# Two early output stores in a tuned cumsum-difference matmul: issued ahead of the next transposes instead of last

## The chip, the cores and the metric

The kernel runs on one core of a Trainium2 chip. The metric is the device time of one execution in microseconds (us), lower is better. The kernel before takes 1458.15 us, the median of three runs that lie between 1458.01 and 1458.67 us.

## The reference, cut to what matters

```python
cs = np.cumsum(x, axis=1)                       # x: 8 x 2048 x 2048, float32
diff = cs - np.concatenate([zeros, cs[:, :-1, :]], axis=1)
return np.matmul(diff, w).astype(np.float32)    # w: 2048 x 2048, float32
```

The difference of a running sum is the input again, so the kernel computes x times w: 16384 rows of x, each 2048 long, times one 2048 x 2048 matrix.

## The kernel before, in words

**Tiling.** A row tile is 128 rows of x (x2, lines 112 and 487). There are 128 of them. The output row of a tile has four column blocks of 512; the left half of w has blocks 0 and 1, the right half blocks 2 and 3.

**First part.** Row tiles 0 to 3 are multiplied plainly, in bf16, while w arrives. `fetch` (L258) loads a stripe of w, `cast` (L266) narrows it, `plain` (L303) multiplies. The left half of the four tiles is finished first: `plain_out(0, r)` copies seven results out of PSUM (tile 3 gives one block there, the other comes from `left_over`). The first two, of tile 0, lie in the buffer F. The other five lie in the five `results` buffers o0 to o4: o0 and o1 are tile 1, o2 and o3 tile 2, o4 tile 3. All seven are noted in the list `done`, to be stored later by `put` (L313). Then the right half of w comes in, and its eight results are noted in a second list `done`; the five left-half stores that wait meanwhile are called `stored`.

**Second part.** From row tile 4 on the kernel works on groups of four tiles with sums and products of half and quarter blocks in fp16, so that fewer matmuls are needed. A tile takes these steps: two loads into F (`load`, L112; tile 5 alone comes by one DMA into the space of xP, L487), a sum of absolute values on ScalarE (`weigh`, L124), two tiny VectorE steps (`scale_of`, L141 and L143), narrowing to fp16 on ScalarE (`narrow`, L163), and two DMA transposes (`turn`, L176). Results leave by `keep` (ScalarE, L630) and `add` (VectorE, L633), and by `put` (L644).

**The first group of the second part** is `group_plain`, on tiles 4, 5, 6 and 7, called g, g + 1, h and h + 1 there. TensorE does, each as 16 matmuls of line 603: A11g x B11, A12g x B21, A11h x B11, A12h x B21, then S1g x T1, S2g x T2, S4g x B22, S3g x T3, then the same for h, beginning with S2h x T2. S1g is the sum of the two transposed halves of tile 5; it is made by VectorE (`total`, L593) and written to the tile S1, S2g from S1g and tile 4. S1h and S2h are the same for tiles 7 and 6. T1, T2 and T3 are differences of pieces of w (L505 and L585).

**Memory.** Everything in the block `with ExitStack() as head` gives its space back at the end of the first part. In the order of allocation these are the seven ring buffers of 2 KB per partition, the five results buffers o0 to o4 of 2 KB, and xP. Then the second part allocates in the same space seven buffers c0 to c6 of 2 KB, S1 of 4 KB and `inner` of 20 KB. S1 so lies where o0 and o1 lay, and `inner` where o2 to o4 and most of xP lay. Whoever writes S1 first must wait until the stores that read o0 and o1 have landed.

**The order of the work.** Every DMA of the kernel is issued by SyncE (SP), whose instructions run in the order of the program. The order is written out by hand: `after(engine, ...)` keeps each engine's instructions in the order of the calls. SP's DMAs use eight completion semaphores in turn, so a DMA waits, besides its data, until the DMA eight issues before it has landed. Around the change SP's order is: the last five stripes of w, two loads of tile 6, two stores from F, two transposes of tile 4 (L176), the load of tile 5 (L487), two right-half stores whose buffers are needed soon, two transposes of tile 6, two loads of tile 7, two transposes of tile 5, six right-half stores, the five left-half stores o0 to o4, the store of `left_over`, two loads of tile 8, two stores of tile 4's result, two transposes of tile 7.

Of the kernel before, what the change touches and what calls it, by code (L numbers as in the profile page):

```python
# [10 lines left out]
def kernel(  # L11
# [96 lines left out]
    def load(t, i):  # L108
        if t < END:
            after(  # L110
                "sp",
                lambda: nc.sync.dma_start(  # L112
                    where[t][i], x2[ds(t * P, P), ds(i * NH, NH)]
                ),
            )
# [69 lines left out]
    with ExitStack() as head:  # L185
# [126 lines left out]
        def put(c, rows, columns, queue=nc.gpsimd):  # L312
            return queue.dma_start(out2[rows, columns], c)  # L313
# [45 lines left out]
        done = []  # L359
# [76 lines left out]
            bring(ko)  # L436
        load(PLAIN + 2, 0)
        load(PLAIN + 2, 1)
        for c, rows, columns in done[:2]:
            put(c, rows, columns, nc.sync)  # L440
        stored = done[2:]
        done = []
        greatest_of_w(1)
        scale_of_w(1)
# [857 lines left out]
```

## Time and profile before

| what | value |
|---|---|
| median of three runs | 1458.15 us |
| the profiled execution, its own time | 1456.43 us |
| its span in the trace | 1454.4 us |
| mean granted TensorE clock | 0.998 |
| TensorE matmul busy | 1441.0 us |
| VectorE busy | 1318.1 us |
| ScalarE busy | 972.1 us |
| share of the 16 DMA engines of the one DMA queue that SP feeds | 86.0% |
| stores from the buffers o | 5, of 256 KB each, median 4.4 us from issue to landing |

The profile shows one execution of the program. PE is TensorE (PEld its weight loads), DVE VectorE, ACT ScalarE, POOL GpSimd, SP SyncE; SPq is the sequencer of SP, which issues the DMAs. A row of the timeline has the start in us from the start of the span, the duration, the engine, the line of the kernel, the operation, the tile written and the tile read, and how many instructions were merged; in brackets stands how long the engine was idle before and what ended that. A tile is named without its number: `o` stands for any of o0 to o4, `x` for any transposed half tile, `S` for S1. The chain of waits follows the work back from the last instruction to what released each step.

### The profile page before, as it was taken

How to read it: one execution, taken by the hardware profiler on the slowest of the kernel's cores; microseconds unless marked ns; L12 is line 12 of the kernel's file. 1: busy time of each engine (PE TensorE's matmuls, PEld its weight loads, DVE VectorE, ACT ScalarE, POOL GpSimd, SP SyncE). 2: the span in 40 equal slices, each digit the busy share in tenths (PEclk: the TensorE clock that was granted, in tenths of full speed). 3: DMA queues.
4: the chain of work that ended last, by engine and by line, in shares of the span. 5: the costliest groups of instructions: out<-in, count | busy, mean ns of one | idle time of the engine just before them, and what ended most of it. 6: DMA issues, size and time to landing. Idle time of an engine off the chain costs nothing.

```text
span 1454.4 us, 20187 instructions
## 1 busy us (share of the span) xinstructions
PE 1441.0 (99%) x6692; PEld 652.2 (45%) x6692; DVE 1318.1 (91%) x2309; ACT 972.1 (67%) x1473; POOL 42.9 (3%) x130
## 2 busy tenths in 40 slices
PE   8989999999999999999999999999999999999998
PEld 4434444444444444444444444444444444444443
DVE  5888899999999999999999999999999999999998
ACT  6967566676666666667666667766666766666662
POOL 0011000000000000000000000000000000000000
PEclk9999999999999999999999999999999999999999
DMA  9999788998888998878998888988878988889973
GB/s 364 345 253 291 200 214 238 249 247 234 234 232 241 246 253 230 237 236 232 260 242 231 219 242 239 261 234 243 227 232 244 250 238 235 229 241 247 254 201 124
DMA packets 378199, 351.58 MB, mean 242 GB/s; under 512 B 274800, under 2 KB 274800, under 8 KB 377968
## 3 DMA queue, kind: packets, MB, share of 16 engines
q1 hardware_dynamic: 378096, 350.31, 86.0%
q8 instruction: 52, 0.85, 0.2%
q14 instruction: 51, 0.42, 0.1%
HBM read 150.99 MB, written 134.22 MB: 196 GB/s over the span
## 4 chain that ended last, share of the span: by engine, by line
PE 93%; DMA 2%; DVE 2%; issue 1%; ACT 1%; SPq 0%; DVEq 0%; POOL 0%; ACTq 0%
PE b L622 61%; PE b L603 32%; DMA W<-in_w_dram 2%; ACT waste L272 1%; DVE c L633 1%; DVE W L341 0%; DMA out_dram<-o 0%; DVE W L505 0%; SPq L224 0%; ACT o L331 0%; DVE wb L333 0%; DVE x L333 0%; DVE W L585 0%; ACT F L163 0%; SPq L313 0%
## 5 line engine op out<-in xcount | busy, mean ns | idle before, releaser
L633 DVE SCALAR_TENSOR_TENSOR c<-b,of,c 128x512 f32<-128x512 f32 x790 | 573.6, 746 | 73.5 <-PE b L622 63.6
L603 PE MATMUL b<-W,x 128*128 128x512 f16 x2144 | 506.6, 379 | 0.0
L630 ACT ACTIVATE c<-b,of 128x512 f32<-128x512 f32 x492 | 313.2, 680 | 228.4 <-PE b L622 117.2
L622 PE MATMUL b<-W,x 128*128 128x512 f16 x1904 | 455.1, 379 | 0.0
L163 ACT ACTIVATE F<-F,of 128x1024 f16<-128x1024 f32 x246 | 282.3, 1148 | 178.6 <-DVE of L143 176.4
L622 PEld LDWEIGHTS <-x 128*128 128x128 f16 x2500 | 244.6, 98 | 295.9 <-issue 1.9
L603 PEld LDWEIGHTS <-x 128*128 128x128 f16 x2144 | 209.8, 98 | 253.0
L124 ACT ACTIVATE waste<-F 128x1024 uint8<-128x1024 f32 x246 | 259.2, 1054 | 4.8 <-DMA F<-in_x_dram 2.7
L622 PEld LDWEIGHTS <-inner 128*128 128x128 f16 x1644 | 160.9, 98 | 194.0
L622 PE MATMUL b<-W,inner 128*128 128x512 f16 x940 | 241.2, 379 | 0.0
L593 DVE TENSOR_TENSOR x<-x,x 128x1024 f16<-128x1024 f16 (+1 forms) x390 | 227.2, 583 | 3.2
L622 PE MATMUL b<-flow,x 128*128 128x512 f16 x588 | 150.9, 379 | 0.0
L622 PE MATMUL b<-inner 128*128 128x512 f16 x472 | 121.1, 379 | 0.0
L946 DVE TENSOR_TENSOR flow<-W 128x2048 f16<-128x2048 f16 x88 | 107.0, 1216 | 0.0
L1039 DVE TENSOR_TENSOR b<-b,c 128x512 f32<-128x512 f32 x116 | 80.4, 694 | 13.4 <-PE b L622 13.4
L149 POOL TENSOR_SCALAR of<-uw,of 128x2 f32<-128x2 f32 x124 | 41.7, 350 | 1307.1 <-DVE of L141 734.7
L946 DVE TENSOR_TENSOR flow<-W,inner 128x2048 f16<-128x2048 f16 x58 | 70.8, 1220 | 0.0
L1032 ACT COPY c<-b 128x512 f32<-128x512 f32 x58 | 33.4, 577 | 51.6 <-PE b L622 49.7
L303 PE MATMUL b<-wb,xP 128*128 128x512 bf16 x240 | 54.0, 379 | 2.0 <-DVE wb L266 1.3
L1032 ACT COPY b<-b 128x512 f32<-128x512 f32 x87 | 51.2, 589 | 0.0
L593 DVE TENSOR_TENSOR inner<-x 128x512 f16<-128x512 f16 x117 | 49.3, 421 | 2.0
L593 DVE TENSOR_TENSOR inner<-x,inner 128x512 f16<-128x512 f16 x117 | 49.2, 421 | 2.0
(66 smaller groups left out, 518.7 us busy)
## 6 DMA issues: line engine op xcount, KB each, us to landing
F<-in_x_dram SPq DMA_DIRECT2D x246, 512.0 KB, 5.2
out_dram<-c SPq DMA_DIRECT2D x492, 256.0 KB, 3.0
W<-in_w_dram SPq DMA_DIRECT2D x32, 512.0 KB, 8.8
W<-in_x_dram SPq DMA_DIRECT2D x16, 256.0 KB, 7.8
x<-F SPq DMA_TRANSPOSE x246, 3.3
out_dram<-wb SPq DMA_DIRECT2D x5, 256.0 KB, 3.5
out_dram<-o SPq DMA_DIRECT2D x5, 256.0 KB, 4.4
xP<-in_x_dram SPq DMA_DIRECT2D x1, 1024.0 KB, 4.8
```

What stands on the lines that cost most here:

```text
L124: lambda: nc.scalar.activation(waste, where[t][i], ABS, scale=1.0 / ROW, accum_out=sums_of[t][:, i : i + 1],),
L149: after("pool", lambda: nc.gpsimd.tensor_scalar(u, uw, m, None, MUL))
L163: lambda: nc.scalar.activation(narrowed(t)[:, ds(i * NH, NH)], where[t][i], COPY, scale=s),
L303: lambda: nc.tensor.matmul(ps[r][n], xP[:, r, ko, :], wb[h, ko][:, ds(n * NB, NB)], start=(ko == 0), stop=(ko == KO - 1),),
L593: after("dve", lambda: nc.vector.tensor_tensor(dst.all, p.all, q.all, op))
L603: said = nc.tensor.matmul(to[n], a[k], b[k][:, n, :], start=(first and k == 0), stop=(k == KH - 1), skip_group_check=True,)
L622: said = nc.tensor.matmul(to, a[k], b[k], start=(first and k == 0), stop=(k == 3), skip_group_check=True)
L630: after("act", lambda: nc.scalar.activation(c, p, COPY, scale=u))
L633: after("dve", lambda: nc.vector.scalar_tensor_tensor(c, p, u, c, MUL, ADD))
L946: after("dve", lambda: nc.vector.tensor_tensor(in_twos(flow), x, y, op))
L1032: after("act", lambda: nc.scalar.copy(c, p))
L1039: after("dve", lambda: nc.vector.tensor_tensor(t, p, s, ADD))
```

## The change

Of the seven left-half results, the kernel before stores two right after the loads of tile 6 and the five others at the end of the first part. The kernel after stores four there and three at the end. The two that move are o0 and o1. No other instruction changes its place on any engine.

```diff
         load(PLAIN + 2, 0)
         load(PLAIN + 2, 1)
-        for c, rows, columns in done[:2]:
+        for c, rows, columns in done[:4]:
             put(c, rows, columns, nc.sync)
-        stored = done[2:]
+        stored = done[4:]
         done = []
         greatest_of_w(1)
         scale_of_w(1)
```

The list `stored` is issued at the end of the first part, unchanged:

```python
        stores(done[:3] + done[5:] + stored)
        left_over(bank(2))
```

## The prediction

> **What bounds the kernel now.** I read the page first: who is busy, and which engine the chain of waits runs on.
>
> ```profile
> PE 1441.0 (99%) x6692; PEld 652.2 (45%) x6692; DVE 1318.1 (91%) x2309; ACT 972.1 (67%) x1473; POOL 42.9 (3%) x130
> PE 93%; DMA 2%; DVE 2%; issue 1%; ACT 1%; SPq 0%; DVEq 0%; POOL 0%; ACTq 0%
> ```
>
> TensorE is the bound: 1441.0 of 1454.4 us busy, 93% of the chain. So only time in which TensorE stands still, or runs slowly, can be won. The second view is that of the waits, for TensorE alone (total, times, longest).
>
> ```profile
> PE b L603 <- DVE S L593: 3.8, 1, 3.8
> PE b L303 <- DVE wb L266: 1.3, 2, 1.1
> ```
>
> One wait is larger than all others: 3.8 us, once, for VectorE's tile S. The next, 1.3 us, belongs to the plain products at the start. The third view, the chain in order of time, shows where the 3.8 us come from.
>
> ```profile
> 83.47 0.63 SPq L313
> ...
> 84.15 4.46 DMA out_dram<-o
> ...
> 88.62 0.70 DVE S L593
> ...
> 89.38 43.30 PE b L603 x192
> ```
>
> SP issues the stores of o0 (83.47) and o1 (next), o1 lands at 84.15 + 4.46 = 88.61, VectorE then writes S, and TensorE goes on. S lies where o0 and o1 lay. Had S covered o2 also, it would have had to wait for a third, later store. Last come TensorE's own rows and its granted clock (the column after POOL; the last two are DMA share and GB/s).
>
> ```profile
> 71.58 13.98 PE L603 MATMUL b<-W,x 128*128 128x512 f16 x64
> 89.38 5.31 PE L603 MATMUL b<-W,S 128*128 128x512 f16 x16 [3.82 <-DVE S L593]
> 94.53 13.98 PE L603 MATMUL b<-W,x 128*128 128x512 f16 x64
> ```
>
> ```profile
> 90.00:91.00 1.00, 1.00 (x5) 0.45 (x4) 0.93 (x4) 0.00 (x0) 0.01 (x1) 0.80 1.11 219
> ...
> 93.00:94.00 1.00, 1.00 (x4) 0.34 (x3) 1.00 (x2) 1.00 (x3) 0.00 (x0) 0.50 0.98 383
> 94.00:95.00 1.00, 1.00 (x6) 0.43 (x5) 1.00 (x3) 1.00 (x3) 0.00 (x0) 1.00 1.00 389
> ```
>
> The gap costs more than itself. 64 matmuls take 13.98 us with the tail of the last one; with 0.38 us for one matmul in flight and 63 steps that is 0.2158 us a step. After the gap 16 matmuls take 94.53 - 89.38 = 5.15 us, where 16 x 0.2158 = 3.45 us would do: the clock is at half from within the slice 90 to 91 to the end of slice 93.
>
> **The change part by part.** It adds and removes no instruction. Two stores of 256 KB leave the row of stores at 83.47 and go in behind the two stores from F; on SP they are moved past two transposes of tile 4, the load of tile 5, two stores, the transposes of tiles 6 and 5, the loads of tile 7 and six stores.
>
> *What it takes away.* With o0 and o1 landed long before, S waits for its inputs and its place on VectorE only. The inputs are the transposes of tile 5.
>
> ```profile
> 75.56 4.33 SPq L176 DMA_TRANSPOSE x<-xP  x2
> DMA to landing us min/median/max: 4.8/5.0/5.4
> 82.41 0.67 DVE L585 TENSOR_TENSOR W<-W 128x1024 f16<-128x1024 f16 x1
> 88.62 0.69 DVE L593 TENSOR_TENSOR S<-x,x 128x1024 f16<-128x1024 f16 x1 [5.55 <-DMA out_dram<-o]
> ```
>
> The landing row is that of the tile xP (4.8 its load, 5.4 and 5.0 the two transposes). They are issued at 75.56 and about 76.9, so they land at 81.0 and 81.9. VectorE is free at 82.41 + 0.67 = 83.08. S then runs from 83.1 to 83.8, 5.5 us earlier than now. TensorE's 64 matmuls before the gap would be followed without a break at 71.58 + 64 x 0.2158 = 85.39: S is ready 1.6 us ahead. TensorE is at the place where it now is at 94.53 by 85.39 + 3.45 = 88.84. The gain is 94.53 - 88.84 = **5.7 us**: 4.0 us of gap (89.38 - 85.39) and 1.7 us of half clock.
>
> *What it adds at the new place.* SP's order there:
>
> ```profile
> 45.76 4.21 SPq L258 DMA_DIRECT2D W<-in_w_dram  x4
> 50.92 1.60 SPq L112 DMA_DIRECT2D F<-in_x_dram  x2
> 53.52 1.62 SPq L313 DMA_DIRECT2D out_dram<-F  x2
> 58.60 4.88 SPq L176 DMA_TRANSPOSE x<-F  x2
> 64.87 0.34 SPq L487 DMA_DIRECT2D xP<-in_x_dram  x1
> DMA to landing us min/median/max: 10.2/10.3/10.3
> 57.44 2.31 ACT L163 ACTIVATE F<-F,of 128x1024 f16<-128x1024 f32 x2
> ```
>
> SP is done with the F stores at 55.14 and idle until 58.60, when narrowing has finished the first half of tile 4 (it begins at 57.44 and takes 1.15 a half). The new stores have to wait for the DMAs eight issues before them, the first two of the four w stripes in row one. These are issued about 1.3 us apart from 45.76 on and land 10.3 us later (the sixth row, which is of these four): 56.1 and 57.3. So the stores are issued at about 56.1 and 57.3, each within 0.4 us as the F stores, and SP is free at 57.7. The transposes of tile 4 now wait for the other two stripes, which land at 58.6 and 59.9; they start at 58.6 and 60.1 as before. Cost on SP: nothing, hidden in 3.5 us of idle time.
>
> The DMA engines have to carry 0.52 MB earlier.
>
> ```profile
> 59.00:60.00 1.00, 1.00 (x6) 0.49 (x5) 1.00 (x3) 1.00 (x2) 0.00 (x0) 1.00 1.05 418
> x<-F SPq DMA_TRANSPOSE x1, 6.0
> ```
>
> At 418 GB/s that is 1.25 us. The first transpose now lands at 58.6 + 6.0 = 64.6 (the second row, KB of a transpose not given), and TensorE uses it at 71.58; 1.25 us later is hidden by 7.0 us. The load of tile 5 may land up to 1.25 us later than its 64.87 + 4.8 = 69.7; from there to S there are 1.6 us to spare at TensorE, and the way between has idle time besides, so I take 0; from below I allow no gain here, from above 1.25 us eaten by those 1.6.
>
> *What is late next.* Everything up to S2g moves 5.5 us ahead with VectorE. The next input that SP brings is tile 7.
>
> ```profile
> 83.47 3.38 SPq L313 DMA_DIRECT2D out_dram<-o  x5
> 86.95 0.59 SPq L313 DMA_DIRECT2D out_dram<-x  x1
> DMA to landing us min/median/max: 5.0/5.0/5.0
> SPq L176 <- DMA out_dram<-x: 2.0, 1, 2.0
> 92.30 4.01 SPq L176 DMA_TRANSPOSE x<-F  x2
> DMA to landing us min/median/max: 4.5/4.7/5.0
> 101.54 0.69 DVE L593 TENSOR_TENSOR x<-S,x 128x1024 f16<-128x1024 f16 x1
> ```
>
> The transposes of tile 7 overwrite the buffer that the `left_over` store reads. That store is issued at 86.95 and lands 5.0 later, at 91.95 (the fourth row is the wait for it); the transposes start at 92.30 and about 93.8 and land 5.0 and 4.5 later, 97.3 and 98.3. S1h, the x sum and S2h follow, 2.2 us of VectorE, and S2h ends at 102.2. TensorE now wants S2h 3 x 3.45 us after 94.53, at 104.9: 2.7 us to spare. After the change it wants it at 88.84 + 10.35 = 99.2. SP reaches the `left_over` store two issues (3.38 x 2/5 = 1.35 us) earlier, at 85.6, with 0.5 MB less in front of it. By the landing of the store that now is issued in that place (85.52, between the 4.5 of o1 and the 5.0 of `left_over`) it lands at 90.0 to 90.6. The transposes then start 1.7 to 2.3 us earlier and land by 96.0 to 96.6, and S2h ends at 98.2 to 98.8. So the spare time shrinks from 2.7 to 0.4 to 1.0 us, but TensorE doesn't stop. Bounds: at best nothing is lost; at worst the transposes land as now at 98.3, S2h ends at 100.5, and TensorE stands still for 1.3 us. I take 0, nearest to the estimate. After that TensorE runs without a stop in the trace of before, and its suppliers wait for it, so I let the gain pass to the end.
>
> *The sum.* Span 1454.4 - 5.7 = 1448.7; with 1456.43 - 1454.4 = 2.03 us around it, 1450.7 us for the profiled execution. That execution is 1.72 us below the median 1458.15 of the runs, so I carry the difference over: 1458.15 - 5.7 = **1452.5 us**, 0.39% faster.
>
> **The rivals.**
>
> *The clock.* The half clock may not be there in every execution. A shorter stop elsewhere leaves it whole:
>
> ```profile
> 26.01 1.24 PE L303 MATMUL b<-wb,xP 128*128 128x512 bf16 x5 [1.06 <-DVE wb L266]
> 26.00:27.00 1.00, 0.99 (x5) 0.48 (x5) 0.45 (x1) 0.97 (x3) 0.00 (x0) 1.00 1.00 395
> ```
>
> After 1.06 us of standstill the clock is granted in full, after 3.82 us it is halved. If 3.82 us lies at the edge, the timed runs may keep their clock, and the change wins the 4.0 us of gap only: 1458.15 - 4.0 = 1454.2 us. For it: one gap of each size is all the trace has. Against it: the three runs agree within 0.66 us, less than the 1.7 that the clock costs, so they all have it or all lack it. The Trainium skill, TensorE: Matmul & The Clock Gate, section on the HAM clock gate, says that the clock is halved after an idle window of about 3.4 us and that the window runs freely, whatever the kernel does. By that rule a gap of 3.8 us holds a whole window in some executions only, and the gain would be 4.0 or 5.7 by chance; the two gaps here agree with its threshold, and nothing here shows the chance.
>
> *A wait that takes the place.* The tile 7 transposes are late, as bounded above: a new stop of up to 1.3 us ahead of S2h x T2. That stop is near the 1.06 us that left the clock whole. Time 1452.7 to 1453.8. For it: the DMA engines are full in the slices after 90, and transposes queue behind loads there. Against: SP comes to them earlier and with less in front.
>
> *It doesn't do what it says.* S takes its first write only after o2 too, or VectorE waits for something with the same date. With o2's store in the place of o0's and a landing as o0's or o1's (3.8 to 4.5 us after 83.47) S starts at 87.3 to 88.0, and the gain is 0.6 to 1.3 us: 1456.9 to 1457.6 (1.7 less if the shorter gap leaves the clock whole). Against: sizes (4 KB of S on two buffers of 2 KB), and S was released by the second store, not by the third.
>
> *Slower.* The two stores stand in front of the transposes of tile 4 and the load of tile 5, on engines that are full (share 1.05). If stores and transposes hold that load up, tile 5 is late and S with it. It lands at 69.7 now; S runs at 88.62 now and its inputs are there at 81.9. So the load may come 6.7 us later before S is later than today; from there each us costs one, and slower by 0.2% (2.9 us) takes 9.6 us. For it: of the 4.88 us of the two transposes' issue most is the second's, so SP is held up there already. Against: 0.52 MB take 1.25 us. At 10 us of delay: 88.62 would be 91.9, 1461.5 us.
>
> **How the numbers follow.** Forecast 64%; clock 12%; tile 7 late 12%; without effect 6%; slower 6%. The predicted time is 1452.5. Its own uncertainty is the spread of the runs (0.66 us) on either side and the 0.4 us between ways of counting the gap (3.82 idle or 4.0 by starts), so 1451.4 at the low end. The high end takes in the clock (1454.2) and the tile 7 stop (1453.8) with the same spread: 1455.0. That leaves the last two cases out, 12%. About 0.2% (2.9 us) is what a measurement of this kernel can tell from no change. Faster by over 0.2%: 64 + 12 + 12 = 88%; within 0.2%: 6%; slower: 6%.
>
> **What would show it.** Right: the row of S starts at about 83.1 with no idle time ended by a store of o; TensorE has no idle time before its first S matmuls, which start at about 85.4, and the clock stays at 1.00 in the slices 85 to 95; the second half of tile 4's transposes still starts at about 60; the tile 7 transposes start at about 90 and TensorE's S2h x T2 at about 99.2 without idle time; the span is 5.7 us shorter. Wrong: VectorE waits before S for a transpose of xP (tile 5 late) or for a store; a new idle time of TensorE between 85 and 110; or a gain at 95 us that is given back later, where the trace would show waits of TensorE that it doesn't have now.

## The result and the profile after

| | before | after |
|---|---|---|
| median (lowest to highest), 11 runs each | 1457.42 us (1455.11 to 1458.67) | 1453.58 us (1452.38 to 1453.90) |
| the profiled execution, its own time | 1456.43 us | 1453.9 us |
| its span | 1454.4 us | 1451.9 us |
| mean granted TensorE clock in it | 0.998 | 1.000 |

The change makes the kernel 3.84 us faster; the ratio is 0.9974, 95% interval 0.9964 to 0.9983. The forecast was 5.7 us. The two profiles differ by only 2.5 us, because the profiled execution of before lies 1.0 us below its median and that of after 0.3 us above. So I read from the profiles where time goes, and from the medians how much.

TensorE in the first group of the second part, in the timeline of the kernel after:

```profile
71.84 13.98 PE L603 MATMUL b<-W,x 128*128 128x512 f16 x64
85.65 3.62 PE L603 MATMUL b<-W,S 128*128 128x512 f16 x16
89.11 3.62 PE L603 MATMUL b<-W,x 128*128 128x512 f16 x16
94.03 0.38 PE L603 MATMUL b<-W,x 128*128 128x512 f16 x1 [1.31 <-ACT inner L630]
94.61 10.38 PE L603 MATMUL b<-W,x 128*128 128x512 f16 x47 [0.20 <-ACT inner L630]
104.82 3.62 PE L603 MATMUL b<-W,S 128*128 128x512 f16 x16
```

The stop before S is gone: the 64 matmuls are followed at once at 85.65, and the 16 take 3.62 us, not 5.31. S2g x T2 starts at 89.11 instead of 94.53, 5.4 us earlier, although this execution had reached the 64 matmuls 0.26 us later. That is the forecast 5.7. But the next 16 matmuls, S4g x B22, meet a new stop, recorded as 1.31 + 0.20 = 1.51 us of idle time. S1h x T1 comes 64 matmuls after 89.11; at 0.2158 us each it would start at 102.92, and it starts at 104.82, so by starts the stop is 1.9 us. S1h x T1 is thus only 3.5 us earlier than in before (108.34).

What releases the new stop is ScalarE's row, and behind it is a store. The rows are those of ScalarE, and of VectorE for S1g, S1h and S2h:

```profile
92.14 2.42 ACT L630 ACTIVATE inner<-b,of 128x512 f32<-128x512 f32 x4 [2.76 <-DMA out_dram<-o]
83.87 0.69 DVE L593 TENSOR_TENSOR S<-x,x 128x1024 f16<-128x1024 f16 x1 [0.58 <-issue]
99.09 0.69 DVE L593 TENSOR_TENSOR S<-x,x 128x1024 f16<-128x1024 f16 x1 [3.73 <-DMA x<-F]
100.61 0.69 DVE L593 TENSOR_TENSOR x<-S,x 128x1024 f16<-128x1024 f16 x1
```

S4g x B22 writes the PSUM bank that ScalarE must first copy to `inner`; `inner` lies where o2 to o4 lay, and the last of these, issued at 86.71, lands 5.3 us later, at 92.0. VectorE waits as well: at S1h, 3.73 us, for the transposes of tile 7. That makes S2h, the last row, ready at 101.30, which is when TensorE comes to it (31 matmuls of 0.2158 us after 94.61): the second chain is as late as the first, and only hidden by it. The stores and transposes that are late stand in SP's timeline:

```profile
56.29 1.61 SPq L313 DMA_DIRECT2D out_dram<-o  x2
58.86 6.46 SPq L176 DMA_TRANSPOSE x<-F  x2
65.41 0.54 SPq L487 DMA_DIRECT2D xP<-in_x_dram  x1
76.27 5.47 SPq L176 DMA_TRANSPOSE x<-xP  x2
81.79 1.54 SPq L313 DMA_DIRECT2D out_dram<-wb  x3
85.34 2.01 SPq L313 DMA_DIRECT2D out_dram<-o  x3
87.44 0.59 SPq L313 DMA_DIRECT2D out_dram<-x  x1
92.48 4.50 SPq L176 DMA_TRANSPOSE x<-F  x2
```

The two stores go out in SP's idle time, as forecast, and the transposes start on time at 58.86. But their issue takes 6.46 us (4.88 before), that of tile 5's 5.47 (4.33). The late list begins at 81.79 instead of 79.94, so the 1.35 us that the shorter list saves are lost: the `left_over` store is issued at 87.44 (86.95 before) and the transposes of tile 7 start at 92.48 (92.30 before).

In the view by windows the stretch after the old stop shows how full the engines are; the last two columns are the share of the 16 DMA engines' time and the GB/s, first after, then before:

```profile
95.00:105.00 10.00, 10.00 (x47) 4.39 (x46) 6.09 (x12) 5.38 (x9) 0.29 (x1) 1.00 0.89 223
```

```profile
95.00:105.00 10.00, 10.00 (x48) 4.56 (x47) 9.83 (x18) 6.59 (x10) 0.29 (x1) 1.00 0.70 181
```

Before had room there (0.70), after has less (0.89). I read this as the transfers that the old stop gave time to and that are now still under way; the view doesn't name them.

Later there are small waits that before did not have, here two of TensorE and one of VectorE:

```profile
133.00 1.02 PE L622 MATMUL b<-W,inner 128*128 128x512 f16 x4 [0.24 <-DVE c L633]
167.74 1.89 PE L622 MATMUL b<-W,x 128*128 128x512 f16 x8 [0.25 <-ACT b L1032]
130.33 0.69 DVE L593 TENSOR_TENSOR S<-x,x 128x1024 f16<-128x1024 f16 x1 [1.52 <-DMA x<-F]
```

The last matmuls of the program start at 1445.77 instead of 1448.25, 2.5 us earlier: of 3.5 us at 108 us another 1.0 us is given back, nearly all before 175 us.

### The profile page after: what moved, and what is told of

Read it like the earlier page. It is cut to its first block, busy times and chain, and to the rows that moved or that the text cites. A ratio compares the mean times of both kernels' runs of the same rounds, so it can differ in the third digit from the quotient of the medians.

```text
span 1451.9 us, 20188 instructions
## 1 busy us (share of the span) xinstructions
PE 1439.1 (99%) x6686; PEld 651.5 (45%) x6692; DVE 1318.2 (91%) x2309; ACT 971.3 (67%) x1473; POOL 43.8 (3%) x130
## 3 DMA queue, kind: packets, MB, share of 16 engines
q1 hardware_dynamic: 378096, 350.31, 86.9%
## 4 chain that ended last, share of the span: by engine, by line
PE 93%; DMA 4%; DVE 2%; issue 1%; ACT 0%; SPq 0%; DVEq 0%; ACTq 0%
PE b L622 60%; PE b L603 31%; DMA W<-in_w_dram 4%; DVE c L633 1%; PE b L303 0%; DMA x<-F 0%; DVE x L593 0%; PE b L457 0%; DMA out_dram<-c 0%; DVE W L341 0%; DVE wb L266 0%; ACT F L163 0%; ACT inner L630 0%; SPq L224 0%; SPq L258 0%
```

## The experiments

Theory 1 was that two chains are late together (the stores of o2 to o4 that `inner` waits for, the transposes of tile 7 that S1h waits for); theory 2 that the wait for `inner` alone gave back the gain; theory 3 that the two stores hold up SP from their new place. Theory 4 came after the first four runs: the DMA engines are full from 75 to 100 us (in after their share is 0.90 from 75 to 80 us and 1.00 to 1.19 in the four stretches of 5 us that follow), so that a transfer which is helped only puts another one late. In the table the third column is the idle time of TensorE before S, the fourth that at a later place of the first group (S4g x B22 or S2h x T2), the fifth the start of S1h x T1.

| kernel | profile: span | before S | later stop | S1h x T1 | median us | ratio to before, 95% |
|---|---|---|---|---|---|---|
| before | 1454.4 | 3.82 | none | 108.34 | 1457.42 | 1 |
| after | 1451.9 | none | 1.51, S4g | 104.82 | 1453.58 | 0.9974 (0.9964 to 0.9983) |
| after again | 1451.9 | none | 1.62, S4g | 104.61 | 1453.62 | 0.9976 (0.9966 to 0.9986) |
| rest first | 1451.5 | none | 1.60, S2h | 104.52 | 1453.47 | 0.9975 (0.9964 to 0.9985) |
| left_over first | 1451.1 | none | 1.30, S2h | 104.55 | 1453.46 | 0.9976 (0.9966 to 0.9986) |
| without o0, o1 | 1450.5 | none | none | 102.78 | 1453.31 | 0.9973 (0.9962 to 0.9983) |
| before, rest first | 1452.3 | none | 1.88, S2h | 104.48 | 1454.38 | 0.9979 (0.9971 to 0.9988) |
| before, middle | 1451.1 | 1.74 | none | 104.82 | 1453.69 | 0.9974 (0.9965 to 0.9984) |
| before, later | 1458.4 | 6.41 | none | 112.14 | 1459.97 | 1.0016 (1.0007 to 1.0025) |
| no late stores | 1449.3 | none | none | 103.17 | 1451.09 | 0.9957 (0.9945 to 0.9970) |
| half a load later | 1451.0 | none | none | 103.11 | 1453.77 | 0.9976 (0.9967 to 0.9986) |
| idle slot | 1450.5 | 0.40 | 0.28, S2h | 104.04 | 1452.59 | 0.9969 (0.9958 to 0.9981) |
| idle slot, more | 1451.6 | 0.83 | none | 105.68 | 1453.90 | 0.9981 (0.9972 to 0.9990) |

The runs of before beside them had medians of 1457.06 (with the first four experiments, in the order of the sections below), 1457.40 (the next four) and 1456.68 (the last three). They differ by 0.7 us, so times from different groups are to be compared by their ratios to before.

### Rest first

```diff
-        stores(done[:3] + done[5:] + stored)
+        stores(stored + done[:3] + done[5:])
```

> The changed kernel, with the three stores o2 to o4 at the head of the late list of stores instead of its end. Theory 1 (two chains end together: the write to inner that waits for o2 to o4, and S2h that waits for the transposes of tile 7): ScalarE writes inner at about 89.3 us without waiting for a store, TensorE runs on into S4g x B22 at about 92.6, but the left_over store is issued as late as now (87.4), the transposes of tile 7 start at about 92.5 as now, S2h ends at about 101.3, and TensorE, which would want it at 99.5, stands still there for about 1.8 us. Time as the changed kernel, 1453.6 within 0.6 us. Theory 2 (the wait for inner alone gave back the gain): no idle time of TensorE between 85 and 110 us, time 1.9 us below the changed kernel, about 1451.7 us.

The rows of TensorE and of SP:

```profile
101.05 3.63 PE L603 MATMUL b<-W,x 128*128 128x512 f16 x16 [1.60 <-DVE x L593]
92.41 4.25 SPq L176 DMA_TRANSPOSE x<-F  x2
```

Theory 1 as it stands, theory 2 is out: the stop at S4g is gone, and one of the same length stands before S2h x T2. The time is the same (1453.47).

### left_over first

```diff
-        stores(done[:3] + done[5:] + stored)
-        left_over(bank(2))
+        left_over(bank(2))
+        stores(stored + done[:3] + done[5:])
```

> As the run before this one, and the left_over store ahead of all late stores. Theory 1: the transposes of tile 7 no longer wait for that store but for their narrowing, so they start at about 88.5 to 90 us instead of 92.5 and land by about 96; S2h ends at about 98.3, before TensorE wants it at 99.5; o2 to o4 land by about 88.5. No idle time of TensorE over 0.3 us between 85 and 110 us; 1.5 to 1.9 us below the changed kernel, 1451.7 to 1452.1 us. Theory 2 (inner alone): the same time as the run before this one. A third possibility, that the DMA engines are full and the transposes land late wherever they are issued: S2h still ends after 100.5 and nothing is won over the run before this one.

SP's row of the transposes of tile 7 and TensorE's row, and from the view of their source line the times from issue to landing:

```profile
90.19 6.56 SPq L176 DMA_TRANSPOSE x<-F  x2
101.08 3.63 PE L603 MATMUL b<-W,x 128*128 128x512 f16 x16 [1.30 <-DVE x L593]
```

```profile
DMA to landing us min/median/max: 5.9/6.8/7.6
```

The same line in after:

```profile
DMA to landing us min/median/max: 4.9/5.2/5.6
```

They are issued 2.3 and 1.4 us earlier and land after 7.6 and 5.9 us, 0.3 us earlier than in after (97.8 and 98.7, against 98.1 and 99.0); the time stays (1453.46). My theory 1 expected 1.5 to 1.9 us here and failed: the third possibility held. Here the earlier issue didn't bring an earlier landing.

### Without o0 and o1

```diff
-        for c, rows, columns in done[:4]:
+        for c, rows, columns in done[:2]:
             put(c, rows, columns, nc.sync)
         stored = done[4:]
```

> The changed kernel without the two moved stores: o0 and o1 are not stored at all, so the left half of row tile 1 is missing in the output. It prices the stores at their new place. Theory 3 (the two stores hold up the transposes of tiles 4 and 5 and SP behind them by about 1.9 us): the issue of the second transpose of tile 4 takes about 3.3 us instead of 4.4, the first late store is issued at about 80.0 instead of 81.8 us, o4 lands at about 90 instead of 91.9, the wait of ScalarE for it falls from 2.8 to about 0.9 us and TensorE's stop from 1.5 us idle to under 0.3. Time 1.5 to 1.9 us below the changed kernel, 1451.7 to 1452.1. If the lateness of SP is only the scatter between executions: first late store at about 81.8, stop as now, time 1453.6 within 0.5 us.

SP's rows, and ScalarE's wait in the view of the waits (us in all, how many, the longest):

```profile
58.72 4.85 SPq L176 DMA_TRANSPOSE x<-F  x2
80.01 1.54 SPq L313 DMA_DIRECT2D out_dram<-wb  x3
```

```profile
ACT inner L630 <- DMA out_dram<-o: 0.8, 1, 0.8
```

Theory 3 holds in the profile: issue 4.85 us, list at 80.01, wait 0.8, no stop, S1h x T1 2.0 us ahead of after. So the moved stores do cost at their new place what the rows of after showed. But the time it expected, 1.5 to 1.9 us below after, is missed: the profile's span is 1.4 us below that of after, the median only 0.3 us and the ratio to before the same (0.9973, 0.9974), which these runs don't tell from zero. Taking away the stop at S4g alone is not shown to win anything. More is given back after 108 us: S1h x T1 is 5.6 us ahead of before, the last matmuls (1444.25) 4.0.

### Before, rest first

```diff
-        stores(done[:3] + done[5:] + stored)
+        stores(stored + done[:3] + done[5:])
```

> The kernel before, with all five stores of o at the head of the late list instead of its end; none is moved ahead of the transposes. Theory 1: the place ahead of the transposes of tile 4 is not needed: o1 is issued at about 80.5 and lands at about 84, S is written by 84.7, before TensorE wants it at 85.4; no half clock; inner doesn't wait; S2h is late as in the first run here, a stop of about 1.5 us. Time 5.7 - 1.5 = 4.2 us below the kernel before, as the changed kernel. The rival (on full engines a store issued behind the tile 5 transposes lands too late): o1 lands at 86 to 87, TensorE stands still 1 to 2 us before S, and the gain over the kernel before is 2 to 3 us.

VectorE's row of S1g and TensorE's of S2h x T2:

```profile
84.28 0.69 DVE L593 TENSOR_TENSOR S<-x,x 128x1024 f16<-128x1024 f16 x1 [1.37 <-DMA out_dram<-o]
101.02 3.63 PE L603 MATMUL b<-W,x 128*128 128x512 f16 x16 [1.88 <-DVE x L593]
```

S still waits for a store, but only until 84.28 and TensorE doesn't notice. The place ahead of the transposes is not needed for that; the order within the late list brings 1454.38, most of the gain. The profile is that of theory 1, the time is not: 2.7 us below before, where theory 1 said 4.2 and its rival 2 to 3. Up to S1h x T1 the profile is that of rest first; behind it TensorE stops once more, for 1.13 us, where rest first has 0.45. Why this order does so is open.

```profile
168.10 1.89 PE L622 MATMUL b<-W,x 128*128 128x512 f16 x8 [1.13 <-ACT b L1032]
```

### Before, middle

```diff
-        stores(done[:3] + done[5:] + stored)
+        stores(done[:3] + stored + done[5:])
```

> The kernel before, with the five stores of o behind the first three late stores, so that o1 is issued at about 82 us instead of 84. It makes TensorE's stop before S shorter than in the kernel before without taking it away, and so separates the stop from the half clock. o1 lands at about 86, S is written by 87, TensorE stands still for about 1.2 us idle (1.6 by starts). Theory (only the long stop halves the clock, as 1.06 us of idle time does not): the clock stays at 1.00 in the slices 85 to 97, the 16 matmuls after the stop take 3.6 us, and the time is 5.7 - 1.6 = 4.1 us below the kernel before, less what is late behind it (S2h, 0 to 1 us, and about 1 us after 110 us): 2 to 4 us below. Rival (any stop before S halves the clock): 5.3 us for the 16 matmuls and 0.5 to 2.3 us below the kernel before.

TensorE's rows, and the row of its clock for the microsecond in which it is partly granted in before (1.00 is the figure ahead of 1.27 and 254):

```profile
87.55 3.63 PE L603 MATMUL b<-W,S 128*128 128x512 f16 x16 [1.74 <-DVE S L593]
91.01 13.98 PE L603 MATMUL b<-W,x 128*128 128x512 f16 x64
```

```profile
90.00:91.00 1.00, 1.00 (x6) 0.42 (x5) 1.00 (x3) 0.97 (x2) 0.53 (x1) 1.00 1.27 254
```

After a stop of 1.74 us the clock stays whole. And a kernel that keeps 1.74 us of the old stop has the time of the changed kernel, 1453.69, and the same date for S1h x T1, 104.82: that stop takes the place of the new one.

### Before, later

```diff
-        stores(done[:3] + done[5:] + stored)
+        stores(done[:3] + done[5:] + stored[2:] + stored[:2])
```

> The kernel before, with o0 and o1 as the last two of the five instead of the first two. o1 is issued at about 86.2 us and lands at about 91, so TensorE stands still about 2.4 us longer, 6.2 us. Theory (the price is the stop one for one and a fixed piece at half clock): the half clock lasts 3.4 us as in the kernel before and the time is 2.4 us above the kernel before, less what the suppliers give back by having more time (0 to 1 us): 1.4 to 2.4 us above. Rival (the half clock lasts the longer, the longer the stop): 3 us above or more. If the stop were not what sets the time: no change.

TensorE's row in the timeline, and three rows of the view by windows (the granted clock is the figure ahead of the last two):

```profile
92.19 6.30 PE L603 MATMUL b<-W,S 128*128 128x512 f16 x16 [6.41 <-DVE S L593]
```

```profile
90.00:91.00 1.00, 0.00 (x0) 0.00 (x0) 0.00 (x0) 0.00 (x0) 0.00 (x0) 0.90 1.14 223
91.00:92.00 1.00, 0.00 (x0) 0.00 (x0) 0.56 (x1) 0.00 (x0) 0.00 (x0) 0.50 1.13 207
97.00:98.00 1.00, 1.00 (x5) 0.35 (x4) 1.00 (x2) 0.43 (x1) 0.00 (x0) 0.68 0.98 183
```

The stop is 2.6 us longer and the time 2.6 us (1459.97 against 1457.40), just above the 1.4 to 2.4 that the theory said and below the rival's 3. The half clock did grow, from 3.4 us to 6.8 (from within 90 to 91 to within 97 to 98), against the theory; but a part of it now falls into the stop, and the 16 matmuls take 6.13 us from start to start, 1.0 more than in before. So the profiles show 3.6 us and the medians 2.6, and the equality of stop and time is not one for one. The spans differ by 4.0, but this profile lies 0.5 us above its median and that of before 1.0 below; what the half clock is in the other executions no trace shows.

### No late stores

```diff
-        stores(done[:3] + done[5:] + stored)
         left_over(bank(2))
```

> The changed kernel without the nine late stores (six results of the right half and o2, o3, o4 are not stored, so these parts of the output are missing); the left_over store stays. It takes 2.4 MB from the DMA engines between 80 and 92 us. Theory 4 (what is given back between 85 and 175 us is given back because the DMA engines are full and inputs land late): no stop of TensorE over 0.3 us between 85 and 110 us, the transposes of tile 7 land by 95, and between 110 and 175 us no idle time of TensorE at all; 1.9 + 1.0 us below the changed kernel, about 1450.7 us. Rival (a chain of steps on ScalarE and VectorE is late there, whatever the DMA engines do): no stop before 110 us, but the waits after 110 us are there as in the run without o0 and o1 (about 1.3 us by starts against the kernel before), time about 1452 to 1453.

The line of the landing of tile 7's transposes, and TensorE's row (its line numbers are one less here):

```profile
DMA to landing us min/median/max: 3.1/3.2/3.2
```

```profile
89.36 13.98 PE L602 MATMUL b<-W,x 128*128 128x512 f16 x64
```

With 2.4 MB less to carry the same transposes land after 3.2 us, TensorE runs through from 72.09 to 115 us without a stop, and nothing is given back after that: the view of TensorE's waits has none after the plain products. 1451.09 us, every run (1450.54 to 1451.52) below every run of after. This is 6.3 us below before by the medians and 5.3 by the two profiled executions: the forecast 5.7 is there when these nine stores need not be carried. Theory 4 as expected, its rival out. One thing this run leaves together: the nine stores are gone from the DMA engines and from SP's list as well, and `left_over` goes out at 81.43 instead of 87.44. For the engines speaks left_over first, where it goes out as early and the transposes land as late as in after.

### Half a load later

```diff
 # on the run with left_over first
         load(g + 4, 0)
-        load(g + 4, 1)
         product(X, A11g, B11, True)
...
         turn(h + 1)
+        load(g + 4, 1)
```

> The run with the left_over store ahead of all late stores, and the second load of tile 8 behind the transposes of tile 7 instead of ahead of them. In that run the transposes were issued at 90.2 and 92.8 us, 2.2 us earlier than in the changed kernel, and landed at 97.8 and 98.7 all the same. Theory 4 (they land when the transfers ahead of them have been carried): with 0.5 MB less ahead they land 1.3 to 1.6 us earlier, S2h ends at about 99.7 instead of 101.0, and TensorE's stop falls from 1.3 us to 0 to 0.3; 0.5 to 1.3 us below the changed kernel, 1452.3 to 1453.1, if the second load of tile 8 isn't late now in its place, which would show as idle time of VectorE before line 141 at about 100 us. Rival (the transposes have a price of their own, not that of what is ahead): landing and stop as before, 1453.5 us.

TensorE's row of S1h x T1 and VectorE's new wait:

```profile
103.11 3.62 PE L603 MATMUL b<-W,S 128*128 128x512 f16 x16
100.79 0.21 DVE L141 TENSOR_SCALAR of<-of 128x1 f32<-128x1 f32 x1 [1.97 <-ACT waste L124]
```

The transposes land 2.1 us earlier (at 95.7 and 96.6 instead of 97.8 and 98.7; 1.3 to 1.6 expected, but they were also issued 0.5 and 1.2 us earlier), the stop is gone, S1h x T1 is 1.4 us earlier. But the load that was put behind is late now: VectorE waits 1.97 us at line 141, as I had named it, and the time is the same, 1453.77. That this late load is what gives the gain back is likely, but no run shows it alone.

### After again

The changed kernel itself, without an edit.

> The changed kernel again, unaltered, beside the two others of this call. All theories: 1453.5 within 0.6 us. What is asked is whether the stop of its profile (1.5 us idle before S4g x B22, waiting for ScalarE's write to inner) is there in a second execution: the theory that inner and the transposes of tile 7 are late together lets it be there or stand before S2h x T2 instead, 1.3 to 2.0 us in all, with the transposes of tile 7 starting at about 92.4 us.

TensorE's rows of S4g x B22, and ScalarE's:

```profile
93.89 0.38 PE L603 MATMUL b<-W,x 128*128 128x512 f16 x1 [1.42 <-DVE W L585]
94.47 10.30 PE L603 MATMUL b<-W,x 128*128 128x512 f16 x47 [0.20 <-ACT inner L630]
92.00 2.42 ACT L630 ACTIVATE inner<-b,of 128x512 f32<-128x512 f32 x4 [2.86 <-DMA out_dram<-o]
```

The stop stands in the same place, 1.62 us. The releaser named for its first part is another, an instruction of VectorE that ends at about the same time as ScalarE's third copy (92.00 and three quarters of 2.42); ScalarE again waits 2.9 us for a store of o before `inner`.

### Idle slot

```diff
-        stores(done[3:5])
+        stores(stored + done[3:5])
...
-        stores(done[:3] + done[5:] + stored)
+        stores(done[:3] + done[5:])
```

on the kernel before, so that all five go out behind the load of tile 5.

> The kernel before, with all five stores of o right behind the load of tile 5, at about 65.5 to 68 us. SP is idle there until about 70.2 us, and the DMA engines have nothing to do from 69 to 71 us. Theory 4 (the gain is given back because the DMA engines are full between 80 and 100 us): 1.3 MB fewer are carried there, S doesn't wait, inner doesn't wait, the late list ends 3 us earlier, the left_over store is issued at about 84 us and the transposes of tile 7 start at about 89 to 90 and land by 96.5; TensorE's stops between 85 and 110 us fall to 0 to 0.5 us; 1.0 to 2.0 us below the changed kernel, 1451.5 to 1452.5 us. Rival (the stores are only pushed in front of other transfers that are as urgent): the transposes of tiles 6 and 5 start or land 1.5 us or more later, S is written after 85 us, and the time is the changed kernel's, 1453.5 us, or above.

The timeline's rows of SP, of VectorE's S1g and of TensorE's products with S1g and S2h:

```profile
65.61 2.99 SPq L313 DMA_DIRECT2D out_dram<-o  x5
77.72 5.71 SPq L176 DMA_TRANSPOSE x<-xP  x2
85.56 0.69 DVE L593 TENSOR_TENSOR S<-x,x 128x1024 f16<-128x1024 f16 x1 [2.17 <-DMA x<-xP]
86.31 3.63 PE L603 MATMUL b<-W,S 128*128 128x512 f16 x16 [0.40 <-DVE S L593]
100.57 3.63 PE L603 MATMUL b<-W,x 128*128 128x512 f16 x16 [0.28 <-DVE x L593]
```

Both sides had a part. The five stores use idle time of SP and of the DMA engines, but tile 5's transposes come 1.5 us later than in after (2.2 later than in before) and S with them, 0.4 us too late. 1452.59 us, just above the 1451.5 to 1452.5 of theory 4 and 1.0 us below the changed kernel that ran beside it; the ranges of the runs (1451.59 to 1454.01, and 1452.56 to 1454.19) overlap, so that it is faster is likely and not certain.

### Idle slot, more

```diff
-        stores(stored + done[3:5])
+        stores(stored + done[:5])
...
-        stores(done[:3] + done[5:])
-        left_over(bank(2))
+        left_over(bank(2))
+        stores(done[5:])
```

on the kernel of the idle slot.

> As the run before this one, with three of the right-half results stored in that place too (2.1 MB in all) and the left_over store at the head of the late list, which then has four stores. Theory 4: nearly what the run without the nine late stores showed (1451.1 us): no stop of TensorE over 0.3 us between 85 and 110 us, transposes of tile 7 start at about 88.5 to 89.5 us, waits of TensorE between 110 and 175 us under 0.3 us in all; 1451.0 to 1452.0 us. Rival: SP is held up at the third of these results, whose copy ends at about 68.7 us, and the transposes of tile 6 and tile 5 are pushed back by the 2.1 MB (5 us at 400 GB/s, of which the engines have about 2.5 us idle): S late, a stop before S of 1 us or more, 1453 to 1455 us.

TensorE's rows:

```profile
80.49 7.08 PE L603 MATMUL b<-W,x 128*128 128x512 f16 x32 [1.54 <-DMA x<-F]
88.41 3.63 PE L603 MATMUL b<-W,S 128*128 128x512 f16 x16 [0.83 <-DVE S L593]
```

The rival: 2.1 MB are more than that slot takes. Tile 6 is late, then tile 5; 1453.90.

## Why the prediction was right, and where it was not

- *What bounds the kernel; what the change takes away.* Right. S started at 83.87 (83.1 said), TensorE went on without a stop, the clock stayed whole, S2g x T2 was 5.4 us earlier. The run without late stores, 6.3 us below before, shows that the 5.7 us were sized about rightly where nothing else is late.
- *The cost at the new place, "Cost on SP: nothing", "so I take 0".* The dates of the issues were right (56.1 and 57.3 said, 56.29 and 57.57 measured), the conclusion was not. I let the 1.25 us of data be hidden by slack on TensorE and did not ask how long SP is held while it issues the transposes behind them. Measured: that issue took longer by 1.58 us for tile 4, 0.61 for tile 6 and 1.14 for tile 5. A part of this went into SP's idle time, and its late list began 1.85 us later (0.26 of that is the later start of this execution); all of it is gone in the run without these stores.
- *What is late next.* The step that failed. I took 0 for it, within 0 to 1.3 us, and followed one chain, tile 7; S2h was ready at 101.3, not at 98.8, for the `left_over` store did not come earlier. And I did not follow `inner`, although it lies on o2 to o4: that stop came first, 1.5 us idle, 1.9 by starts. The rival of a wait that takes the place had the right kind at 12%, with the wrong tile at its head. Its time (1452.7 to 1453.8) holds the measured 1453.58, its gain (4.35 to 5.45) does not hold the measured 3.84.
- *"I let the gain pass to the end."* Wrong by 1.0 us in the profile: with TensorE ahead, inputs of the next group are late between 110 and 175 us. Without the nine late stores this vanishes too, so these stores are shown as the cause; that it is by way of the DMA engines and not of SP's list is argued for this stretch.
- *The clock.* The rival that the timed runs all keep their clock falls, but the half clock isn't the same in all of them. Of the 66 executions of before beside the experiments, 20 have a mean granted clock of 0.997 (1457.22 to 1458.86 us), 34 have 0.998, as the profiled one, 9 have 0.999 and 3 have 1.000 (1455.41 to 1456.12 us); all 21 of after have 0.999 or 1.000. So a few executions of before seem to have no half clock, and some of the 20 more of it than the 3.4 us of the trace (before, later, with 6.8 us of it, has 0.997 too): the chance that this rival spoke of is there. How much of the measured gain it makes is open, since one execution of before was traced. In the traces, stops of 1.06 and 1.74 us left the clock whole, 3.82 and 6.41 us halved it. The Trainium skill, TensorE: Matmul & The Clock Gate, section on the HAM clock gate, puts the limit at about 3.4 us; the four stops agree.
- *The sum.* 5.7 forecast, 3.84 measured: by the profile's terms 5.4 (5.7 less a later start of 0.26), less 1.9 between 89 and 108 us, less 1.0 after it, is 2.5, the difference of the spans. The 1.3 us between that and the medians is the position of the two profiles among their runs. How the medians' 3.84 divides is not shown: in the runs without o0 and o1 and half a load later the stop between 89 and 108 us is gone, and their ratios to before (0.9973 and 0.9976) are still that of after. Shown is the whole: with the nine late stores away it is 6.3 instead of 3.84. My bounds for "what is late next" covered one chain instead of what both chains wait for.
- *What was luck.* The time came out 1.1 us above 1452.5, the gain 1.9 us below 5.7. The difference is the base: 1458.15 was the median of three executions, and eleven gave 1457.42. From there the same working gives 1451.7 with a range of 1450.7 to 1454.3, which still holds 1453.58, but further up.

## What to carry to other kernels

When a stop of the bounding engine is taken away, the transfers around it must be carried in a time that is shorter by just that stop: before crediting the gain, add up the bytes that lie between the stop and the next stretch with idle DMA engines. Here, moving one transfer forward mostly chose which other one was late: four of the orders tried (after, rest first, left_over first, before middle) gave 1453.46 to 1453.69, while before, rest first gave 1454.38 and before, later 1459.97. The one order that was likely better, the idle slot with 1452.59, used a stretch in which the engines have little to do (share 0.05 from 69 to 71 us in before), and more than fits there lost it again (1453.90).

## What the runs showed of the hardware

- Issuing a transpose on SP takes a time that varies, and everything behind it in SP's order waits as well. Of the 246 transposes from F in after (least, median and most in ns):

```profile
L176 SPq DMA_TRANSPOSE x<-F x246: 1231/1282/4382, 58.9 to 1413.3; - x123
```

  The longest is the second one of tile 4, 60.93 to 65.31; in the run without o0 and o1, with 0.5 MB less ahead of it, it took 3.32 us. That full engines lengthen it is not shown as a rule: the DMA queue is 86.9% busy over the whole run, and the median is near the least.
- From issue to landing the transposes of tile 7 took 3.2 us (no late stores), 5.2 (median in after) and up to 7.6 us (left_over first, issued up to 2.3 us earlier than in after and landed 0.3 us earlier).
- The half clock lasted 3.4 us after a stop of 3.82 us, all of it on matmuls, and 6.8 us after one of 6.41. Worked out from the shares of the slices at its ends (0.80 and 0.50 in before, 0.90 and 0.68 in before, later), it began at 90.6 and 90.8 us, in both about 5.0 us after the last matmul before the stop (85.56 and 85.78).
